# Layer 0's last stage with an interleaved order for VectorE and ScalarE, and the first values by pairs of token tiles

## The chip, the cores and the metric

The kernel runs on one core of a Trainium2 chip. The metric is the device time of one execution in microseconds; the median of several runs is compared.

## What is computed

Two layers of a decoder over 512 tokens with 1024 features, in 32-bit floats. Layer 0 mixes tokens by windowed attention and a short convolution, layer 1 by gated linear attention (GLA). Each layer then has a gated MLP and a per-layer embedding, which is the stage in question for layer 0:

```python
def _per_layer_embedding(x, p_i, norm, w_gate, w_proj):
    gate = jax.nn.sigmoid(_rms_norm(x, norm) @ w_gate)
    return gate * (p_i @ w_proj)

x = x + _per_layer_embedding(x, p[i], ...)          # end of layer 0
h = _rms_norm(x, mix_norm[1])                        # begin of layer 1
q, k, v, g_lr, og = _split(h @ w_in, GLA_SPLITS)
```

## The kernel before

Features lie on the 128 partitions: `xT[0..7]` are eight tiles of 128 features by 512 tokens. TensorE multiplies in a format that keeps only the upper part of a number, so every operand is cut in two: ScalarE writes the rounded part (`h`, an ACTIVATE Copy), VectorE the rest (`l = x - h`, a TENSOR_TENSOR subtract), and a product takes three matmuls (h·h, h·l, l·h). `mm3_rests_last` does those that need the weights' rest after all the others, so that the rest may come later.

`ple0` is layer 0's per-layer embedding. Its gate's weight matrix is worked in four groups of 256 output features (`for g in range(groups)`). A group's product with the tokens is made by a scheme of seven block products instead of eight: VectorE forms differences of the weight blocks in place in `raw` (`first_forms` L874 and L875, `second` L1410, `fourth` L1413), and `cut_blocks` (L850 ScalarE, L851 VectorE) cuts each form as it is ready. Per group there are four cuts: `plain`, `t13`, `t2` and `last`. The products build up in three PSUM banks: `bank` (from `pa`, its right half becomes `more`), `X` and `Y` (from `ps`). ScalarE copies one bank into another where a sum is used twice (L1420, L1421, L1487, L1503). `proj` multiplies p by its own weights into `pa` banks, two for a group. There are four `pa` and four `ps` banks.

The gate of a group is finished one group later (`late`): `closing` scales X and Y by the row norm R (L1428 to L1430, VectorE), `sigmoids` (L1435, ScalarE), `closed` multiplies by the projection (L1439, which frees its `pa` bank) and adds to `xT` (L1442). `squares` then prepares the next norm (L307, L311 ScalarE, L312 VectorE into `acc`). After the loop the last group is closed, `enter` scales and cuts the `xT` tiles for layer 1 (L113 ScalarE, L114 VectorE), and `cut` (L151, L152) cuts the first two weight blocks of the GLA values, `first_values`.

Inside `ple0` the order on TensorE, VectorE and ScalarE is the order in which the code is written (`manual_schedule`): each engine takes its instructions in that order and waits at each for what it needs. Outside, in `mixer1`, a planner orders each engine's instructions by its own costs; its order is fixed when the kernel is built.

`mixer1` begins with `Values(...).step(0)` and `step(1)`: the products of the eight token tiles with the two first weight blocks into four `ps` banks, one for each 128 tokens, all matmuls without the weights' rest ahead of those with it. Then come `spread` (R by transposes, L369), copies of the values out of PSUM (L1760, L1761, ScalarE), and `query(w, 0, turn_low)`, whose weights are cut by L151 and L152 and which calls `turn_low` (transposes of the gate's low rank, L1827) ahead of its last two feature tiles. `gate_up` loads the gate's small matrix `wgu` by ScalarE's DMA queue into the buffer that `acc` had, and rounds it (L1819, L1820). `acc` is summed by four transposes (L351) and a reduction (L360).

Of the kernel before, what the change touches and what calls it, by code (L numbers as in the profile page):

```python
# [63 lines left out]
class Kernel:  # L64
# [69 lines left out]
    def cut(self, rv, by, offs=(0, 0)):  # L134


        nc = self.nc
        na, nb = rv.shape[1:]
        parts = []
        n = 2 if na * nb > 1024 else 1  # L140
        for k in range(n):
            if by == "b":
                a, b = na, nb // n
                v = rv[:, :, k * b : (k + 1) * b]
            else:
                a, b = na // n, nb
# [4 lines left out]
            nc.scalar.activation(hv, v, AF.Copy)  # L151
            self.rest_cut = nc.vector.tensor_tensor(lv, v, hv.bitcast(F32), ALU.subtract)  # L152
            parts.append((hv, lv))
# [21 lines left out]
    def mm3_rests_last(self, terms, start, stop, weights, **kw):  # L175


        mm = self.nc.tensor.matmul
        begun, left = set(), {}
        for out, lt, rt in terms:  # L180
            left[id(out)] = left.get(id(out), 0) + 1
        for out, (lh, ll), (rh, rl) in terms:
            first = start and id(out) not in begun
            begun.add(id(out))
            mm(out, lh, rh, start=first, stop=False, **kw)  # L185
            lt, rt = (lh, rl) if weights == 0 else (ll, rh)
            mm(out, lt, rt, start=False, stop=False, **kw)  # L187
        for out, (lh, ll), (rh, rl) in terms:
            left[id(out)] -= 1
            lt, rt = (ll, rh) if weights == 0 else (lh, rl)  # L190
            mm(out, lt, rt, start=False, stop=stop and not left[id(out)], **kw)  # L191
# [648 lines left out]
    def cut_blocks(self, src, wide=True):  # L840

        nc = self.nc
        if wide:
            h, l = self.weight_tiles(BLOCKS)
        else:
            h, l = (
                self.sp.tile([P, S + 64], F32R, tag="sq", name=self.nm("t2"), bufs=2)[:, o : o + S] for o in BLOCKS
            )
        h, l = (x.rearrange("p (j n) -> p j n", n=src.shape[2]) for x in (h, l))
        nc.scalar.activation(h, src, AF.Copy)  # L850
        nc.vector.tensor_tensor(l, src, h.bitcast(F32), ALU.subtract)  # L851
# [521 lines left out]
    def ple0(self, fp, both, gain, next_gain):  # L1373
# [34 lines left out]

        def second(ev, od):
            tt(ev[:, :, :P], od[:, :, P:], ev[:, :, :P], ALU.subtract)  # L1410
# [4 lines left out]
        def begun(plain, rests_last):  # L1415
# [3 lines left out]
            X, Y = self.ps(), self.ps()  # L1419
            copy(X[:, left], bank[:, left])  # L1420
            copy(Y[:, left], bank[:, left])  # L1421
            return X, Y, bank[:, right]

        def closing(X, Y, more):
            gates = both()
            h2 = lambda x: x.rearrange("p (u t) -> p u t", u=2)
            g0, g1 = gates[:, 0], gates[:, 1]
            tt(g0, X, R, ALU.mult)  # L1428
            tt(h2(g1), h2(Y), more.unsqueeze(1).to_broadcast([P, 2, H]), ALU.add)
            tt(g1, g1, R, ALU.mult)  # L1430
            return g0, g1

        def sigmoids(gates):
            for s in gates:
                nc.scalar.activation(s, s, AF.Sigmoid)  # L1435

        def closed(g, gates, pjs):
            for s, pj in zip(gates, pjs):
                tt(s, s, pj, ALU.mult)  # L1439
            for c, s in enumerate(gates):  # L1440
                m = 2 * g + c
                tt(self.xT[m], self.xT[m], s, ALU.add)  # L1442
# [6 lines left out]
        with tc.manual_schedule(engines={ET.PE, ET.DVE, ET.Activation}):  # L1449
# [19 lines left out]
            X, Y, V = begun(plain, False)  # L1469
# [6 lines left out]
            for g in range(groups):  # L1476
                ends = g + 1 == groups
                product(V, t13, 0, x["s1"], False, g > 0)
# [3 lines left out]
                if g == 0:  # L1482
                    for m in (6, 7):
                        self.squares(m, spare())
                last = self.cut_blocks(od)
                product(Y[:, left], t2, 0, x["s2"], False, g > 0)
                copy(X[:, right], Y[:, left])  # L1487
                if late:
                    gates = closing(*late[1])
# [5 lines left out]
                else:  # L1495
                    pjs = [proj(2 * g), proj(2 * g + 1)]
                if not ends:
# [5 lines left out]
                copy(Y[:, right], X[:, right])  # L1503
                done = late
                if late:
                    closed(late[0], gates, late[2])
                late = g, (X, Y, more), pjs
                bank = X, Y
# [10 lines left out]
                product(bank[1][:, left], last, 1, x["s4"], False, g > 0)  # L1519
                product(bank[0][:, right], last, 0, x["o2"], False, g > 0)  # L1520
                if g == 0:
                    R = self.spread()
                if not ends:
                    if g + 2 < groups:
                        following = load(g + 2)
                    second(ev, od)
                    t2 = self.cut_blocks(ev[:, :, :P], False)
                    fourth(ev, od)
            raws = []
# [3 lines left out]
            ws = [self.cut(raws[0], "a")]  # L1533
            gates = closing(*late[1])
            sigmoids(gates)
            closed(late[0], gates, late[2])
            enter(4, 5)
            for m in (6, 7):
                self.squares(m, spare())
            ws.append(self.cut(raws[1], "a"))  # L1540
            enter(6, 7)
            self.first_values = ws
# [185 lines left out]
    def mixer1(self):  # L1728
# [4 lines left out]
        with tc.tile_pool(name="m1", bufs=1) as mp:  # L1733
# [5 lines left out]
            class Values:  # L1739


                def __init__(v, c0, c1, vn, ws=None):
                    v.c0, v.n, v.vn = c0, c1 - c0, vn
                    v.ws = ws or [
# [3 lines left out]
                def step(v, i):  # L1748
                    c0, n, vn = v.c0, v.n, v.vn
                    if i == 0:  # L1750
                        v.pss = [self.ps() for _ in range(NT)]
                    outs = [x[:, :n] for x in v.pss]
                    terms = [
                        (outs[t], tok(k, t), v.ws[i](k % 4, 0, n)) for k in range(4 * i, 4 * i + 4) for t in range(NT)
                    ]
# [12 lines left out]
            def feature(w, c, amid=None):  # L1768
# [3 lines left out]
                self.mm3_rests_last(terms[:n], True, n == ND, 0)  # L1772
                if amid:
                    amid()
# [428 lines left out]
```

## Time and profile before

| | us |
|---|---|
| median of 3 runs | 1209.86 (1209.41 to 1212.33) |
| the profiled execution | 1209.54 |
| its span in the profile | 1207.8 |
| the stage, from the loop's first product to the first values' product | 524.07 to 583.44 |
| the first values, to the first query's product | 583.44 to 603.47 |

In a timeline a row has the start, the duration, the engine, line and operation, the output and inputs, the shape and the count; in brackets the engine's idle time ahead of it and what ended that. PE is TensorE, DVE VectorE, ACT ScalarE, POOL GpSimd. A row with a count merges neighbours. In the rows of windows each engine has its busy time and instructions, and the last three numbers are the granted TensorE clock as a share, the DMA engines' busy share and GB/s.

### The profile page before, as it was taken

Reading aid. Unit: us, or ns where it says so; the run is one execution under the profiler, and the core shown is the slowest. Engines: PE = TensorE matmul, PEld = TensorE weight load, DVE = VectorE, ACT = ScalarE, POOL = GpSimd, SP = SyncE. Lnnn points to the kernel's source line nnn. Section 1 sums busy time; section 2 is a strip of 40 time slices with the busy share of each in tenths; the row PEclk is TensorE's granted clock in tenths of the full one; section 3 lists DMA queues with packets and bytes.
Section 4 is the critical chain, followed back from the end, with each engine's and each line's share of the span. In section 5 each row is a group of like instructions: output and inputs, shape, how many; then the busy total and the mean of one; then the engine's idle time right before and its main releaser. Section 6 shows DMA issues by size and latency. Waiting matters only on the chain.

```text
span 1207.8 us, 20228 instructions
## 1 busy us (share of the span) xinstructions
PE 1191.7 (99%) x8218; PEld 1083.1 (90%) x8218; DVE 994.7 (82%) x1593; ACT 692.3 (57%) x1137; POOL 45.4 (4%) x64
## 2 busy tenths in 40 slices
PE   9999999999999999998899999999999999999998
PEld 8877789999999889888888988889999999888887
DVE  6786687898999986987879876687989999988595
ACT  7466555656565644754573565555565656645374
POOL 2600000000000000000100000000000000000000
PEclk9999999999999999999999999999999999999999
DMA  7232222323232433321331322223333332422601
GB/s 221 73 102 72 73 88 71 113 98 112 99 106 88 157 122 97 99 68 61 114 93 47 94 71 70 87 70 106 106 106 106 101 110 95 141 88 97 209 1 70
DMA packets 112929, 117.76 MB, mean 98 GB/s; under 512 B 2840, under 2 KB 107858, under 8 KB 112836
## 3 DMA queue, kind: packets, MB, share of 16 engines
q1 hardware_dynamic: 112000, 115.88, 29.8%
q8 instruction: 64, 1.05, 0.4%
q0 software_dynamic: 560, 0.42, 0.3%
q14 instruction: 29, 0.24, 0.1%
q10 hardware_dynamic: 276, 0.18, 0.0%
HBM read 114.37 MB, written 2.10 MB: 96 GB/s over the span
## 4 chain that ended last, share of the span: by engine, by line
PE 85%; DVE 9%; ACT 3%; issue 1%; DMA 1%; POOL 0%; ACTq 0%; DVEq 0%
PE ps L171 8%; PE ps L172 7%; PE ps L173 7%; PE pa L172 6%; PE pa L173 6%; PE pa L171 6%; PE ps L903 5%; PE ps L905 5%; PE ps L904 5%; PE ps L185 4%; PE ps L187 4%; PE ps L191 4%; PE pa L903 2%; PE pa L905 2%; PE pa L904 2%; DVE wl L851 2%
## 5 line engine op out<-in xcount | busy, mean ns | idle before, releaser
L152 DVE TENSOR_TENSOR wl<-raw,wh 128x1024 fp32r<-128x1024 f32 (+4 forms) x142 | 162.4, 1146 | 44.2 <-ACT wh L151 40.7
L151 ACT ACTIVATE wh<-raw 128x1024 fp32r<-128x1024 f32 (+4 forms) x142 | 140.9, 996 | 69.8 <-PE ps L172 28.6
L850 ACT ACTIVATE wh<-raw 128x1024 fp32r<-128x1024 f32 x90 | 95.7, 1063 | 122.8 <-DVE raw L875 79.0
L966 DVE SCALAR_TENSOR_TENSOR zt<-z,vfa,zt 128x510 f32<-128x510 f32 (+1 forms) x176 | 130.8, 744 | 0.3
L851 DVE TENSOR_TENSOR wl<-raw,wh 128x1024 fp32r<-128x1024 f32 x90 | 110.0, 1222 | 24.3 <-ACT wh L850 23.4
L173 PE MATMUL pa<-b,wl 128*128 128x256 f32 x352 | 97.3, 276 | 0.1
L173 PE MATMUL pa<-a,wl 128*128 128x256 f32 x352 | 97.2, 276 | 0.0
L171 PE MATMUL pa<-a,wh 128*128 128x256 f32 x352 | 97.2, 276 | 0.0
L171 PE MATMUL pa<-b,wh 128*128 128x256 f32 x352 | 97.2, 276 | 0.0
L172 PE MATMUL pa<-b,wh 128*128 128x256 f32 x352 | 97.2, 276 | 0.0
L172 PE MATMUL pa<-a,wh 128*128 128x256 f32 x352 | 97.2, 276 | 0.0
L964 ACT ACTIVATE zt<-z,vfb 128x512 f32<-128x512 f32 x88 | 71.3, 810 | 18.1 <-DVE z L956 9.1
L185 PE MATMUL ps<-b,wh 128*128 128x512 f32 (+1 forms) x200 | 76.5, 385 | 0.2 <-ACT vt L1761 0.2
L187 PE MATMUL ps<-b,wh 128*128 128x512 f32 (+1 forms) x200 | 75.2, 379 | 0.0
L173 PEld LDWEIGHTS pa<-b,wl 128*128 128x128 f32 x352 | 66.1, 188 | 0.2 <-DVE wl L152 0.2
L171 PEld LDWEIGHTS pa<-a,wh 128*128 128x128 f32 x352 | 66.1, 188 | 0.0
L171 PEld LDWEIGHTS pa<-b,wh 128*128 128x128 f32 x352 | 66.1, 188 | 0.0
L172 PEld LDWEIGHTS pa<-a,wh 128*128 128x128 f32 x352 | 66.1, 188 | 0.0
L172 PEld LDWEIGHTS pa<-b,wh 128*128 128x128 f32 x352 | 66.1, 188 | 0.0
L173 PEld LDWEIGHTS pa<-a,wl 128*128 128x128 f32 x352 | 66.1, 188 | 0.0
L903 PE MATMUL ps<-four,wh 128*128 128x256 f32 x232 | 64.7, 279 | 0.0
L905 PE MATMUL ps<-four,wl 128*128 128x256 f32 x232 | 64.1, 276 | 0.0
(525 smaller groups left out, 3710.9 us busy)
## 6 DMA issues: line engine op xcount, KB each, us to landing
raw<-in_ffn_w_up_dram SPq DMA_DIRECT2D x42, 1024.0 KB, 5.0
raw<-in_ffn_w_down_dram SPq DMA_DIRECT2D x13, 1024.0 KB, 5.0
raw<-in_hy_w_in_dram SPq DMA_DIRECT2D x8, 1024.0 KB, 5.2
raw<-in_gla_w_in_dram SPq DMA_DIRECT2D x8, 1024.0 KB, 5.2
raw<-in_ffn_w_down_dram SPq DMA_DIRECT2D x8, 768.0 KB, 4.8
raw<-in_ple_w_gate_dram SPq DMA_DIRECT2D x6, 1024.0 KB, 6.5
raw<-in_hy_w_out_dram SPq DMA_DIRECT2D x16, 256.0 KB, 4.1
raw<-in_gla_w_out_dram SPq DMA_DIRECT2D x4, 1024.0 KB, 5.0
```

What stands on the lines that cost most here:

```text
L151: nc.scalar.activation(hv, v, AF.Copy)
L152: self.rest_cut = nc.vector.tensor_tensor(lv, v, hv.bitcast(F32), ALU.subtract)
L171: mm(out, lh, rh, start=start, stop=False, **kw)
L172: mm(out, lh, rl, start=False, stop=False, **kw)
L173: mm(out, ll, rh, start=False, stop=stop, **kw)
L185: mm(out, lh, rh, start=first, stop=False, **kw)
L187: mm(out, lt, rt, start=False, stop=False, **kw)
L850: nc.scalar.activation(h, src, AF.Copy)
L851: nc.vector.tensor_tensor(l, src, h.bitcast(F32), ALU.subtract)
L903: mm(out, wh, xh, start=first and j == 0, stop=False, **kw)
L905: mm(out, wl, xh, start=False, stop=j == ND // 2 - 1, **kw)
L966: nc.vector.scalar_tensor_tensor(out=y[:, tap:], in0=z[:, : S - tap], scalar=w[:, f : f + 1], in1=y[:, tap:], op0=ALU.mult, op1=ALU.add,)
```

## The change

The written order in `ple0` changes, and with it the helpers: `closing`, `sigmoids` and `closed` fall apart into single steps. `cut_blocks` and `cut` take a function `amid` whose instructions stand between ScalarE's rounding and VectorE's rest.

- The late group's first gate multiplication and its sigmoid go into the middle of the cut `last`.
- The multiplications by the projection go ahead of the next group's two first block differences.
- The late group's additions go into the middle of the cut `t13`, and ScalarE's two copies of the new bank go behind that cut's rounding.
- The squares go behind `second`; for the last two tiles behind the last `enter`.
- After the loop, the last group's gate goes into the middle of the first cut of the values' weights.
- `Values.step(0)` of the first values goes over token tiles 0 and 1 for all four features, then 2 and 3. `turn_low` may be issued only after the matmuls written ahead of it.

TensorE's written order in `ple0` stays, and so does the number of instructions. In `mixer1` the planner's order moves in a few places: on ScalarE the rounding of the first query's weights (L151) now stands behind the roundings of `wgu`, all eight copies of the values and the copy of R, where it stood ahead of the copies; on VectorE its rest stands behind the low rank's buffers; on TensorE the four transposes of `acc` stand behind 25 matmuls of `step(1)`, before behind 8, and the four low-rank transposes stand together inside the first query.

```diff
-    def cut_blocks(self, src, wide=True):
+    def cut_blocks(self, src, wide=True, amid=None):
...
         nc.scalar.activation(h, src, AF.Copy)
+        if amid:
+            amid()
         nc.vector.tensor_tensor(l, src, h.bitcast(F32), ALU.subtract)
...
+                if late:
+                    before, (Xb, Yb, mb), pjb = late
+                    gates = both()
+
+                    def amid():
+                        tt(gates[:, 0], Xb, R, ALU.mult)
+                        sigmoid(gates[:, 0])
+                else:
+                    squared(ND // 2 - 1)
-                last = self.cut_blocks(od)
+                last = self.cut_blocks(od, True, amid)
                 product(Y[:, left], t2, 0, x["s2"], False, g > 0)
                 copy(X[:, right], Y[:, left])
                 if late:
-                    gates = closing(*late[1])
+                    summed(gates[:, 1], Yb, mb)
...
                 if not ends:
                     raw, ev, od = following
-                    plain = self.first_forms(ev, od, raw)
+                    plain = self.cut_blocks(raw[:, :, :P])
                 if late:
-                    sigmoids(gates)
+                    sigmoid(gates[:, 1])
+                    for c in range(2):
+                        tt(gates[:, c], gates[:, c], pjb[c], ALU.mult)
+                if not ends:
+                    first_third(ev, od)
                 product(X[:, right], t13, 1, x["s3"], False, g > 0)
                 copy(Y[:, right], X[:, right])
...
                 if ends:
+                    added(before, gates)
                     pjs.append(proj(2 * g + 1))
+                    squared(before)
+                    enter(0, 1, 2, 3)
                 else:
-                    X, Y, V = begun(plain, True)
-                    t13 = self.cut_blocks(ev)
-                if done:
-                    for m in (2 * done[0], 2 * done[0] + 1):
-                        self.squares(m, spare())
-                if ends:
-                    enter(0, 1, 2, 3)
+                    X, Y, bank = begun(plain, True)
+                    t13 = self.cut_blocks(ev, True, (lambda: added(before, gates)) if late else None)
+                    copies(X, Y, bank)
...
                     second(ev, od)
+                    if late:
+                        squared(before)
                     t2 = self.cut_blocks(ev[:, :, :P], False)
                     fourth(ev, od)
...
-            ws = [self.cut(raws[0], "a")]
-            gates = closing(*late[1])
-            sigmoids(gates)
-            closed(late[0], gates, late[2])
+            before, (Xb, Yb, mb), pjb = late
+            gates = both()
+            ws = [self.cut(raws[0], "a", amid=lambda: (tt(gates[:, 0], Xb, R, ALU.mult), summed(gates[:, 1], Yb, mb)))]
+            for c in range(2):
+                sigmoid(gates[:, c])
+                tt(gates[:, c], gates[:, c], pjb[c], ALU.mult)
+            added(before, gates)
             enter(4, 5)
-            for m in (6, 7):
-                self.squares(m, spare())
             ws.append(self.cut(raws[1], "a"))
             enter(6, 7)
+            squared(before)
...
+                    if v.given and i == 0:
+                        order = [(k, t) for u in (0, 2) for k in ks for t in (u, u + 1)]
...
-                    amid()
+                    with tc.issue_after(end.ins):
+                        amid()
```

`added` holds the two additions to `xT`, `squared` the two squares, `summed` the sum with `more` and its scaling by R, `first_third` the two differences that `first_forms` made.

More of the change, by code (lines that the diff above doesn't have):

```diff
@@ L190, in mm3_rests_last @@
             lt, rt = (ll, rh) if weights == 0 else (lh, rl)
-            mm(out, lt, rt, start=False, stop=stop and not left[id(out)], **kw)
+            end = mm(out, lt, rt, start=False, stop=stop and not left[id(out)], **kw)
+        return end
     def rsqrt(self, out, src, scale):
@@ L1418, in begun, with copies, summed, sigmoid @@
             product(bank[:, left], plain, 0, x["e1"], True, rests_last)
-            X, Y = self.ps(), self.ps()
+            return self.ps(), self.ps(), bank
+        def copies(X, Y, bank):
             copy(X[:, left], bank[:, left])
             copy(Y[:, left], bank[:, left])
-            return X, Y, bank[:, right]
-        def closing(X, Y, more):
-            gates = both()
+        def summed(s, Y, more):
             h2 = lambda x: x.rearrange("p (u t) -> p u t", u=2)
[L1427 to L1440, printed above, removed]
+            tt(h2(s), h2(Y), more.unsqueeze(1).to_broadcast([P, 2, H]), ALU.add)
+            tt(s, s, R, ALU.mult)
+        def sigmoid(s):
+            nc.scalar.activation(s, s, AF.Sigmoid)
+        def added(g, gates):
+            for c in range(2):
                 m = 2 * g + c
-                tt(self.xT[m], self.xT[m], s, ALU.add)
+                tt(self.xT[m], self.xT[m], gates[:, c], ALU.add)
+        def squared(g):
+            for m in (2 * g, 2 * g + 1):
+                self.squares(m, spare())
         raw, ev, od = load(0)
@@ L1468, in ple0 @@
                               s3=parts(bh)[0], s4=parts(bh)[1]))
-            X, Y, V = begun(plain, False)
+            X, Y, bank = begun(plain, False)
+            copies(X, Y, bank)
             tt(s34[:, right], o[:, left], s12[:, right], ALU.subtract)
@@ L1477, in ple0 @@
                 ends = g + 1 == groups
+                V = bank[:, right]
                 product(V, t13, 0, x["s1"], False, g > 0)
@@ L1532, in ple0 @@
                 nc.sync.dma_start(raws[-1], wv[:, k0 : k0 + 4, 1696:2064])
-            ws = [self.cut(raws[0], "a")]
-            gates = closing(*late[1])
-            sigmoids(gates)
-            closed(late[0], gates, late[2])
+            before, (Xb, Yb, mb), pjb = late
+            gates = both()
+            ws = [self.cut(raws[0], "a", amid=lambda: (tt(gates[:, 0], Xb, R, ALU.mult), summed(gates[:, 1], Yb, mb)))]
+            for c in range(2):
+                sigmoid(gates[:, c])
+                tt(gates[:, c], gates[:, c], pjb[c], ALU.mult)
+            added(before, gates)
             enter(4, 5)
-            for m in (6, 7):
-                self.squares(m, spare())
             ws.append(self.cut(raws[1], "a"))
             enter(6, 7)
+            squared(before)
             self.first_values = ws
@@ L1743, in __init__ @@
                     v.c0, v.n, v.vn = c0, c1 - c0, vn
+                    v.given = ws is not None
                     v.ws = ws or [
```

36 lines of the change are left out of this document (22 added, 14 removed).

## The prediction

> **What bounds the kernel now.** I read the page's first part, then the chain that ended last, then the stretches of ten microseconds around the stage, then the timeline of each engine inside it.
>
> ```profile
> span 1207.8 us, 20228 instructions
> ...
> PE 1191.7 (99%) x8218; PEld 1083.1 (90%) x8218; DVE 994.7 (82%) x1593; ACT 692.3 (57%) x1137; POOL 45.4 (4%) x64
> ...
> PE 85%; DVE 9%; ACT 3%; issue 1%; DMA 1%; POOL 0%; ACTq 0%; DVEq 0%
> ```
>
> TensorE sets the time: it is busy for 99% of the span, and only 1207.8 - 1191.7 = 16.1 us of idle time exist anywhere. So the change can give only what TensorE idles or crawls in the stretch that it touches, and whatever it takes it takes there. TensorE's rows around that stretch with idle time ahead of them, its last matmuls ahead of the first one, and two of the ten-microsecond windows:
>
> ```profile
> 545.43 0.39 PE L191 MATMUL ps<-b,wl 128*128 128x256 f32 x2
> 547.62 0.39 PE L185 MATMUL pa<-a,wh 128*128 128x256 f32 x1 [1.80 <-DVE zt L1439]
> ...
> 562.89 0.56 PE L185 MATMUL pa<-a,wh 128*128 128x256 f32 x1 [2.66 <-DVE zt L1439]
> ...
> 577.96 0.39 PE L185 MATMUL ps<-a,wh 128*128 128x256 f32 x1 [0.74 <-ACT ps L1503]
> ...
> 583.44 0.67 PE L185 MATMUL ps<-wh,b 128*128 128x368 f32 x1 [2.47 <-ACT wh L151]
> ```
> ```profile
> 560.00:570.00 10.00, 7.34 (x50) 7.13 (x50) 6.99 (x10) 3.31 (x7) 0.00 (x0) 0.83 0.15 56
> ...
> 580.00:590.00 10.00, 7.53 (x39) 7.33 (x38) 9.76 (x16) 7.10 (x12) 0.00 (x0) 0.83 0.15 47
> ```
>
> Four stalls, 7.67 us. The last two rows have the granted clock as the third number from the end: 0.83 over ten microseconds, which at half speed is 3.4 us, so 1.7 us of matmul time is lost behind each of the two longest stalls (2.66 and 2.47), and none behind the 1.80. That is 7.67 + 3.4 = 11.1 us, the most that this change could ever bring. A closed stall gives some 0.16 more than its figure, since idle time is counted from the end of a matmul and the next could start before it (two take 0.39 us, one 0.28).
>
> **The change, part by part.** *Group 2 of the loop.* The stall of 2.66 us ends with VectorE's first multiplication by the projection (L1439), which frees the bank that the next group starts in. VectorE's rows:
>
> ```profile
> 546.89 1.28 DVE L1439 TENSOR_TENSOR zt<-zt,pa 128x512 f32<-128x512 f32 x2
> ...
> 550.95 1.23 DVE L851 TENSOR_TENSOR wl<-raw,wh 128x1024 fp32r<-128x1024 f32 x1 [1.58 <-ACT wh L850]
> 552.09 0.69 DVE L312 TENSOR_TENSOR acc<-acc,so 128x512 f32<-128x512 f32 x1
> 552.69 0.68 DVE L1410 TENSOR_TENSOR raw<-raw 128x512 f32<-128x512 f32 x1
> 554.07 0.69 DVE L851 TENSOR_TENSOR t<-raw,t 128x512 fp32r<-128x512 f32 x1 [0.70 <-ACT t L850]
> 554.68 0.68 DVE L1413 TENSOR_TENSOR raw<-raw 128x512 f32<-128x512 f32 x1
> 556.49 1.23 DVE L851 TENSOR_TENSOR wl<-raw,wh 128x1024 fp32r<-128x1024 f32 x1 [1.13 <-ACT wh L850]
> 557.64 0.68 DVE L1428 TENSOR_TENSOR zt<-ps,R 128x512 f32<-128x512 f32 x1
> 558.24 0.68 DVE L1429 TENSOR_TENSOR zt<-ps,so 128x512 f32<-128x512 f32 x1
> ...
> 560.82 0.69 DVE L874 TENSOR_TENSOR raw<-raw 128x512 f32<-128x512 f32 x1
> ...
> 562.15 1.28 DVE L1439 TENSOR_TENSOR zt<-zt,pa 128x512 f32<-128x512 f32 x2
> ```
>
> L1413 ends at 555.36 and L1439 starts at 562.15: 6.79 us. The gate's first multiplication (L1428, 0.60 from start to start) goes into the 1.13 us wait, and the two block differences (L874 and the next, 562.15 - 560.82 = 1.33) go behind L1439: 6.79 - 0.60 - 1.33 = 4.86 us. From the first L1439 of the group before (546.89, 15.26 us earlier) to L1413's end are 8.47 us. There the two differences come in (+1.33), and two waits nearly go: the 1.58, because ScalarE now rounds before it copies TensorE's new bank, and the 0.70, because the sum of squares (L312) moves into it. 8.47 + 1.33 - 1.54 - 0.65 = 7.6. VectorE's cycle becomes 7.6 + 4.9 = 12.5 us in place of 15.26. TensorE's own work between the two stalls is 562.89 - 547.62 - 2.66 - 0.16 = 12.45. The two tie: the stall falls from 2.66 to about 0 (0 to 0.5, as nothing is spare), and with it the 1.7 us of slow clock.
>
> *Group 1.* The same saving, but the sigmoid's table load comes earlier on ScalarE:
>
> ```profile
> 540.14 1.06 ACT L850 ACTIVATE wh<-raw 128x1024 fp32r<-128x1024 f32 x1 [0.78 <-DVE raw L1413]
> ...
> 543.06 1.28 ACT L1435 ACT_TABLE_LOAD   x1
> 544.35 1.15 ACT L1435 ACTIVATE zt<-zt 128x512 f32<-128x512 f32 x2
> ```
>
> After the rounding (ends 541.20) come the load (1.28), one sigmoid (0.58), the copy for TensorE's next product (0.3, an estimate from half the size of a 0.58 us sigmoid) and only then the next group's rounding (1.06): 544.4. Its rest on VectorE (1.2) and the multiplication (0.68) end at 546.25, against 547.6. The stall falls by 1.4, to 0.4.
>
> *Group 3.* The copy that ends the 0.74 us stall waited behind the second sigmoid; with the gate's first multiplication in VectorE's wait it comes 0.6 us sooner after L1413, and L1413 itself comes sooner by the waits above: closed. The group's other copy now stands behind the first sigmoid, with one projection to cover it instead of two. Counted from L1439's start, L1413 ends at 7.6 + 0.6 (this group adds two sums of squares, not one) = 8.2, the rounding ends at 9.3, the sigmoid at 9.9, the copy at 10.2. TensorE starts at 0.73 and has 72 matmuls at 0.113 (0.39 - 0.28 and a little) and a projection of 1.4 to do, 10.3. So it is covered by 0.1 us; without that cover it would cost up to 0.3.
>
> *Up to the first GLA values.* This stall I expect to stay. Its chain is untouched: additions, squares, four roundings, the weights' rounding, and TensorE.
>
> ```profile
> 578.27 1.29 DVE L1442 TENSOR_TENSOR xT<-xT,zt 128x512 f32<-128x512 f32 x2
> ```
> ```profile
> 580.13 2.55 ACT L113 ACTIVATE b<-xT,vec 128x512 fp32r<-128x512 f32 x4
> 582.58 1.51 ACT L151 ACTIVATE wh<-raw 128x736 fp32r<-128x736 f32 x2
> ```
>
> From the first addition to TensorE's start are 583.44 - 578.27 = 5.17 us. The addition comes 0.6 us sooner after L1413, but TensorE comes out of group 3 sooner as well: 2.4 us of stall against 2.47, and the clock drops again. The order by pairs moves few matmuls (the scheduler had nearly that order) and costs nothing. So the values start at 583.44 - 1.4 - 2.7 - 1.7 - 0.74 - 0.1 - 0.5 (three times 0.16) = 576.3: 7.1 us gained.
>
> *Behind the values: a wait takes the place.* Two things move. The squares of the last two tiles now follow their roundings, so that the transposes that sum them go from 8 matmuls into the second half of the values to 25, and all that hangs on them comes 17 of them later against TensorE: at (2.86 - 0.33) / 15 = 0.17 us each, by the first row below with one matmul's 0.33, 2.9 us. And ScalarE's queue changes: rounding the first query weights stood ahead of the eight copies of the values; in the new order it is behind them, behind two roundings of the gate weights and behind the copy of R.
>
> ```profile
> 590.44 2.86 PE L191 MATMUL ps<-wl,b 128*128 128x368 f32 x16
> ...
> 594.48 0.60 PE L351 MATMUL pa<-cf,acc 128*128 128x128 f32 x4
> ...
> 601.63 0.60 PE L369 MATMUL pa<-cf,rtok 128*128 128x128 f32 x4
> ...
> 603.47 0.50 PE L185 MATMUL ps<-b,wh 128*128 128x512 f32 x1 [0.17 <-ACT vt L1761]
> ```
> ```profile
> 600.44 0.63 ACT L1819 ACTIVATE wgs<-wgu 64x512 fp32r<-64x512 f32 x1 [7.08 <-DMA wgu<-in_gla_w_gate_up_dram]
> 600.98 1.04 ACT L151 ACTIVATE wh<-raw 128x1024 fp32r<-128x1024 f32 x1
> 602.05 0.63 ACT L1820 ACTIVATE wgs<-wgu 32x512 fp32r<-32x512 f32 x1
> 602.70 0.27 ACT L1760 ACTIVATE glr<-ps,rtok 128x16 f32<-128x16 f32 x1
> ...
> 605.08 0.64 ACT L371 COPY R<-pa 128x512 f32<-128x512 f32 x1
> 605.55 2.08 ACT L151 ACTIVATE wh<-raw 128x1024 fp32r<-128x1024 f32 x2
> ```
>
> Call TensorE's spread (601.63) S. The first copy cannot start before the values of tile 0 are complete, S - 0.3. Four copies take half of 605.08 - 602.70, 1.2 us: S + 0.9. There stands the gate weights' rounding, which waits for its load: 600.44 - 595.08 = 5.36 us after the transposes, now at S - 3.9, so S + 1.5. Then 0.54 and 0.63 for the two roundings, 1.2 for the four other copies, 0.5 for R, 1.04 for the query weights: S + 5.4. TensorE's query started at 603.47 - 601.63 = S + 1.84. Loss 3.6 us. TensorE then idles 4.9 us (S + 0.5 to S + 5.4), twice the stalls that cost it its clock, so add 1.7. The gate's low-rank transposes stand together inside the query now, where one stood ahead of it: 0.1 as an estimate.
>
> *Sum.* S comes 7.1 sooner; 7.1 - 3.6 - 1.7 - 0.1 = 1.7 us. The profiled execution took 1209.54 (span 1207.8 and 1.7 around it), the median of the runs is 1209.86. Behind the query the order of all engines is as before and TensorE runs without a gap, so the 1.7 stays: 1207.8 for a profiled execution, 1208.1 against the median.
>
> A rule that weighs on this: the Trainium skill, "TensorE: Matmul & The Clock Gate", section "Why this matters for your kernels", wants no idle gaps over some 3 us, and its section "What's actually happening" tells of a free-running window of 3413 ns. This trace is harsher than the 3 us (2.47 and 2.66 dropped the clock, 1.80 did not), but a window that does not follow the kernel would make the 2.4 us stall a matter of where it falls; that is the second case below.
>
> **The rivals.** *The clock stays up before the values.* 2.4 lies between 1.80 (no drop) and 2.47 (drop). Without a drop 1.7 us more are gained: 1206.4, and with the 0.5 us by which the load's wait could be shorter, 1205.9. For: the stall is the shortest that would still drop. Against: 2.47 is much nearer than 1.80.
>
> *No new wait behind the values.* If ScalarE were through its queue by S + 1.8 the whole 7.1 would stay, 1202.8; half of it 1205. Against: the instructions are in one queue and sum to more than 5 us.
>
> *The gate weights' load decides (slower than before).* ScalarE stands still until that load lands, with the query's weights behind it. Each microsecond beyond S + 1.5 costs one. It breaks even 1.7 us late. Were the load to sit behind one 1 MB load of weights,
> ```profile
> raw<-in_gla_w_in_dram SPq DMA_DIRECT2D x8, 1024.0 KB, 5.2
> ```
> 5.2 us, the time would be 1208.1 + 5.2 = 1213.3. Against: it shared the engines with such a load before, too.
>
> *The stalls stay.* If TensorE's bank is freed by the second multiplication, or ScalarE's new order holds the sigmoid back, groups 1 and 2 keep about a stall of over 2 us with its slow clock: 3 to 4 us less, 1211 to 1212.
>
> **How the numbers follow.** About 0.3% (3.6 us) is what a measurement of this kernel can tell from no change: faster is below 1206.2, slower above 1213.5. Forecast 0.52; clock up 0.22; no new wait 0.08; load 0.08; stalls stay 0.10. Faster: half of the clock case, most of no new wait, some of the forecast's edge, 0.24. Slower: half of the load case and a little of the last, 0.06. Same 0.70. The forecast's own range is 1206.5 to 1209.5; to hold 8 in 10 it reaches to 1205.0 for the clock case and to 1211.5 for the stalls.
>
> **What would show it.** Right: idle before the new group's start under 0.5 us in groups 1 and 2, granted clock 1.00 there; 2.2 to 2.6 us before the values; a gap near 4.9 us before the first query, ended by ScalarE's rounding of its weights, with half clock behind it. Wrong: no such gap, or the stalls by the projection's bank still there.

## The result, and the profile after

The changed kernel takes 1207.84 us (median of 20 runs, 1206.33 to 1210.36), the kernel before 1209.96 (20 runs beside it, 1208.8 to 1212.54). The ratio is 0.998, 95% interval 0.9974 to 0.9987: a gain of 2.1 us, below the 3.6 us that the prediction took as measurable for a single comparison, and shown by the interval all the same. The profiled executions took 1209.54 before and 1207.74 after.

The page's first part and its chain by engines:

```profile
span 1206.0 us, 20223 instructions
...
PE 1189.8 (99%) x8218; PEld 1081.3 (90%) x8218; DVE 995.2 (83%) x1593; ACT 692.8 (57%) x1137; POOL 45.9 (4%) x64
...
PE 85%; DVE 10%; ACT 3%; issue 1%; DMA 1%; POOL 0%; ACTq 0%; DVEq 0%; POOLq 0%
```

TensorE's idle time in the whole span went from 16.1 us to 1206.0 - 1189.8 = 16.2. Nothing was gained there in sum; the gain of 1.8 us in these two executions is in TensorE's busy time (1191.7 to 1189.8), most of it because 3.8 us of its work ran at half clock in place of 6.8. Where the idle time lies is quite another matter. TensorE's timeline (start, duration, and in brackets the idle time ahead and who ended it):

```profile
546.44 0.36 PE L191 MATMUL pa<-a,wh 128*128 128x256 f32 x1 [0.62 <-DVE zt L1524]
...
558.62 0.39 PE L197 MATMUL ps<-b,wl 128*128 128x256 f32 x2
558.86 0.36 PE L191 MATMUL pa<-a,wh 128*128 128x256 f32 x1
...
576.49 0.43 PE L191 MATMUL ps<-wh,b 128*128 128x368 f32 x1 [2.26 <-ACT wh L151]
...
593.14 0.60 PE L376 MATMUL pa<-cf,rtok 128*128 128x128 f32 x4
599.60 0.79 PE L191 MATMUL ps<-b,wh 128*128 128x512 f32 x1 [5.86 <-ACT wh L151]
```

Group 1's stall of 1.80 us is 0.62, group 2's 2.66 has no bracket any more, group 3's is gone, the one before the values is 2.26, and between TensorE's spread (593.14) and the first query there is a new gap of 5.86 us. The clock, as the third number from the end, by stretches:

```profile
560.00:570.00 10.00, 10.00 (x84) 9.74 (x83) 9.30 (x14) 5.55 (x10) 0.00 (x0) 1.00 0.04 4
...
576.00:593.00 17.00, 16.51 (x100) 16.48 (x101) 14.69 (x22) 7.45 (x13) 3.93 (x7) 1.00 0.42 130
593.00:610.00 17.00, 11.14 (x45) 8.55 (x44) 7.10 (x8) 10.74 (x20) 0.00 (x0) 0.80 0.28 89
```

The stretch of group 2's old stall (560 to 570) and the values (576 to 593) ran at full clock; in the last stretch 17 x 0.20 / 0.5 = 6.8 us were at half clock. Read in short windows, that is 596.58 to 603.41: the second half of the gap and the first 3.8 us of the queries. Of the 20 runs the four longest (1208.91 to 1210.36) have a mean granted clock of 0.995, the others 0.996 to 0.998, so in some executions the clock may have dropped once more than in this one.

In balance, by the starts of the same rows: the values begin 583.44 - 576.49 = 6.95 us earlier, the spread 601.63 - 593.14 = 8.49 (the clock did not drop behind the 2.26 us), the first query 603.47 - 599.60 = 3.87. From there to the gate's product it takes 8.59 us in place of 6.69, with the half clock in it, which leaves the 2.0 seen at that product (610.16 before, 608.19 after).

What holds the query, in the chain that ended last (start, length, engine, tile and line):

```profile
587.87 0.70 DVE acc L319
...
588.68 1.01 POOL run L2097
...
590.21 0.46 POOL wgu L1841
590.69 0.32 ACTq L1843
591.04 4.43 DMA wgu<-in_gla_w_gate_up_dram
```

and ScalarE's timeline:

```profile
592.99 0.27 ACT L1787 ACTIVATE glr<-ps,rtok 128x16 f32<-128x16 f32 x1 [8.33 <-PE ps L197]
...
595.48 0.63 ACT L1847 ACTIVATE wgs<-wgu 64x512 fp32r<-64x512 f32 x1 [1.16 <-DMA wgu<-in_gla_w_gate_up_dram]
...
597.99 0.59 ACT L378 COPY R<-pa 128x512 f32<-128x512 f32 x1
598.46 2.03 ACT L151 ACTIVATE wh<-raw 128x1024 fp32r<-128x1024 f32 x2
```

The query weights' rounding (L151 at 598.46) is the last of ScalarE's queue, behind eight copies of the values, a wait for the gate weights' load, two roundings and the copy of R. GpSimd clears two other tiles (from 588.68) before it clears `wgu`, and only then is the load asked for; before, those two were cleared (592.83 to 593.76) ahead of the transposes.

### The profile page after: what moved, and what is told of

It is laid out like the page before. It is cut to its first block, busy times and chain, and to the rows that moved or that the text cites. A ratio compares the mean times of both kernels' runs of the same rounds, so it can differ in the third digit from the quotient of the medians.

```text
span 1206.0 us, 20223 instructions
## 1 busy us (share of the span) xinstructions
PE 1189.8 (99%) x8218; PEld 1081.3 (90%) x8218; DVE 995.2 (83%) x1593; ACT 692.8 (57%) x1137; POOL 45.9 (4%) x64
## 4 chain that ended last, share of the span: by engine, by line
PE 85%; DVE 10%; ACT 3%; issue 1%; DMA 1%; POOL 0%; ACTq 0%; DVEq 0%; POOLq 0%
PE ps L177 8%; PE ps L178 8%; PE ps L179 8%; PE pa L179 6%; PE pa L178 6%; PE pa L177 6%; PE ps L912 5%; PE ps L914 5%; PE ps L913 5%; PE ps L191 4%; PE ps L193 4%; PE ps L197 4%; PE pa L912 2%; PE pa L914 2%; PE pa L913 2%; DVE wl L860 1%
## 5 line engine op out<-in xcount | busy, mean ns | idle before, releaser
L151 ACT ACTIVATE wh<-raw 128x1024 fp32r<-128x1024 f32 (+4 forms) x142 | 140.8, 996 | 70.0 <-PE ps L178 28.5
```

## The experiments

Theory A, the prediction's: the loop's order closes the stalls, and the gain is given back because the squares of the last two tiles, now behind the splits, make the planner put the query weights' rounding last on ScalarE. The rivals: the loop's edits themselves gain little; the pairs order or the call that holds the transposes is what moved the planner's order; or (C) the gate weights' load sets the query's start, whatever the order. The times come from four rounds, each with the kernel before beside it, whose median was 1209.5 to 1210.0; so differences of a few tenths between kernels of different rounds say nothing.

**The multiplications by the projection back behind the block differences.**

```diff
                     sigmoid(gates[:, 1])
-                    for c in range(2):
-                        tt(gates[:, c], gates[:, c], pjb[c], ALU.mult)
                 if not ends:
                     first_third(ev, od)
+                if late:
+                    for c in range(2):
+                        tt(gates[:, c], gates[:, c], pjb[c], ALU.mult)
```

> The changed kernel with the multiplications by the projection behind the next group's two block differences again, all else as changed. Theory A (this order is two thirds of what closes the stalls, 1.33 us of VectorE in each group): the stall of group 1 grows from 0.6 to 1.9, that of group 2 from 0 to about 1.3, no drop of the clock, 1207.8 + 2.6 = 1210.4 us. Theory E (filling VectorE's wait with the gate's first multiplication is what closes them): within 0.7 us of 1207.8.

Measured: 1209.7 (12 runs, ratio to before 1.0, 0.9992 to 1.0009): the whole gain of the change is gone. TensorE's timeline of this kernel:

```profile
547.05 0.55 PE L191 MATMUL pa<-a,wh 128*128 128x256 f32 x1 [2.06 <-DVE zt L1527]
...
561.90 0.35 PE L191 MATMUL pa<-a,wh 128*128 128x256 f32 x1 [0.67 <-DVE zt L1527]
...
578.17 0.44 PE L191 MATMUL ps<-wh,b 128*128 128x368 f32 x1 [0.85 <-ACT wh L151]
```

Group 1's stall returns (2.06, with 3.4 us of half clock behind it), group 2's is 0.67, and the one before the values shrinks to 0.85, since TensorE itself now comes later. Values start 578.17 - 576.49 = 1.7 us later and the medians differ by 1.9, where 2.6 was expected of theory A and under 0.7 of its rival. The total gain is gone, yet not all of the loop's: the values still start 583.44 - 578.17 = 5.3 us earlier than before. So this edit is worth 1.7 of the 6.95 us; which of the loop's other edits brought the rest was not tried one by one. The kernel also shows that one stall hides the next.

**The squares ahead of the second cut.**

```diff
             enter(4, 5)
+            squared(before)
             ws.append(self.cut(raws[1], "a"))
             enter(6, 7)
-            squared(before)
```

> The changed kernel with the squares of the last two tiles put back ahead of the second cut of the values' weights. With that alone the planner's order on ScalarE behind the values is the old one again (the first query's weights are rounded ahead of the eight copies) and the transposes that sum the squares stand behind 8 matmuls of the second half, not 25. Theory A (the queue order behind the values is what takes the gain back, and it hangs on where the squares stand): the gap before the first query falls from 5.9 us to about 1.5, no slow clock behind it, 1207.8 - 4.5 - 1.7 = 1201.5 us. Theory B (the new order in the loop itself makes ScalarE late for the values' copies): the gap stays over 4 us, 1207 us or more.

Measured: 1203.4 (6 runs, ratio 0.9954, 0.9939 to 0.9968), 4.4 us below the changed kernel. ScalarE's timeline, then TensorE's:

```profile
593.20 0.63 ACT L1847 ACTIVATE wgs<-wgu 64x512 fp32r<-64x512 f32 x1 [6.92 <-DMA wgu<-in_gla_gate_bias_dram]
593.74 1.04 ACT L151 ACTIVATE wh<-raw 128x1024 fp32r<-128x1024 f32 x1
```
```profile
596.23 0.50 PE L191 MATMUL ps<-b,wh 128*128 128x512 f32 x1 [0.88 <-ACT vt L1788]
```

The order on ScalarE is the old one again (gate weights, query weights, then the copies) and the query starts 1.5 us behind the spread (594.75) in place of 6.5. The time is 1.9 above the expected: in the profiled execution the clock dropped behind the stall of 2.25 us before the values, which it did not do in the changed kernel's. The times spread from 1202.87 to 1207.64, and why they spread so far is not shown.

**The query weights' load and rounding given priority, and nothing else.**

```diff
-            w = pair_w(0)
+            with tc.high_priority(offset=150):
+                w = pair_w(0)
```

> The changed kernel with a higher priority for the load and the cuts of the first query's weights, nothing else: on ScalarE their two roundings come ahead of all copies of the values, in the middle of the gate weights' five loads; the squares and the transposes stay late, so the load of the gate weights lands as late as before or later. Theory A (the place of the rounding in the queue): the query waits only for the first copy of the values, gap under 1 us, 1207.8 - 5.3 - 1.7 = 1200.8 us. Theory C (the late landing of the gate weights' load is the wait, whatever stands in the queue): the gap stays near 5.9 us and the time within 1 us of 1207.8.

Measured: 1201.76 (5 runs, ratio 0.9932, 0.992 to 0.9944): 6.1 us below the changed kernel. ScalarE and TensorE:

```profile
593.12 1.06 ACT L151 ACTIVATE wh<-raw 128x1024 fp32r<-128x1024 f32 x1 [7.57 <-DVE rs L205]
...
596.66 0.63 ACT L1847 ACTIVATE wgs<-wgu 64x512 fp32r<-64x512 f32 x1 [0.32 <-DMA wgu<-in_gla_w_gate_up_dram]
```
```profile
595.78 0.50 PE L191 MATMUL ps<-b,wh 128*128 128x512 f32 x1 [0.39 <-ACT vt L1788]
```

Here the rounding that waits for the gate weights' load starts 1.9 us behind the spread (594.79; 2.3 in the changed kernel), and the query starts before it, 1.0 us behind the spread. So C falls: the load delays the query only because the query weights stand behind it in ScalarE's queue.

The same line in the kernel before:

> The kernel before, with the query weights' roundings given the same priority that gained 6 us in the changed kernel. Theory: there the queries wait only 1 us in all behind the values (0.79 for the low-rank copy, 0.17 for the values' copy) at full clock, so it gains at most that: 1209.0 to 1209.8. Rival: the priority helps by itself, whatever the loop does: 1204 or less.

Measured: 1210.97 (11 runs, ratio 1.0014, 1.0005 to 1.0023): slower by 1.4 us, outside of what either expected. TensorE, then ScalarE:

```profile
603.62 0.28 PE L1827 MATMUL pa<-cf,glr 128*16 128x128 f32 x1 [1.79 <-ACT glr L1760]
```
```profile
600.62 1.99 ACT L151 ACTIVATE wh<-raw 128x1024 fp32r<-128x1024 f32 x2
```
```profile
600.00:610.00 10.00, 8.05 (x34) 6.29 (x33) 4.69 (x5) 7.12 (x14) 0.00 (x0) 0.83 0.54 173
```

Both halves of the query weights now go ahead of the first low-rank copy, whose transpose stands ahead of the query on TensorE: 0.79 us of waiting became 1.79, and in this execution the clock dropped behind it as well (0.83 over ten microseconds, 1.7 us lost), which it does not do there in the kernel before. (This execution took 1213.87, so it stands for more than the 1.4 us of the median.) The priority is no gain in itself; it mends an order that the change brought about.

**TensorE kept busy in the gap** with 24 products that nothing uses, to price the half clock by itself.

```diff
             R = self.spread()
+            warm = self.pa()
+            for _ in range(24):
+                nc.tensor.matmul(warm, xg[0][0][:, :P], xg[0][0], start=True, stop=True)
             w = pair_w(0)
```

> The changed kernel with 24 matrix products on data already there (128x512, result not used) between the spread and the query weights' first product, to keep TensorE busy through the gap of 5.86 us; the order on every other engine is unchanged. Theory A: of the 4.6 us lost behind the values, the gap itself is the wait for ScalarE's rounding and stays, but the half clock that followed it (3.8 us of work at half speed behind the start of the queries) goes, so 1.8 us less: 1206.0. Rival: the query weights' later halves set the pace there, so that the half clock costs nothing: 1207.8.

Measured: 1204.84 (5 runs, ratio 0.9963, 0.9949 to 0.9976), 3.0 us below the changed kernel where 1.8 was expected. TensorE, and the clock:

```profile
592.94 5.70 PE L2105 MATMUL pa<-b 128*128 128x512 f32 x24
599.04 0.50 PE L191 MATMUL ps<-b,wh 128*128 128x512 f32 x1 [0.40 <-ACT wh L151]
...
601.89 1.53 PE L197 MATMUL ps<-b,wl 128*128 128x512 f32 x6
```
```profile
590.00:600.00 10.00, 9.60 (x49) 8.14 (x48) 2.66 (x4) 6.36 (x14) 2.03 (x4) 1.00 0.35 115
600.00:610.00 10.00, 10.00 (x46) 7.90 (x46) 5.02 (x6) 6.71 (x10) 0.00 (x0) 1.00 0.43 126
```

From the query's start to its first rests are 601.89 - 599.04 = 2.85 us, against 604.22 - 599.60 = 4.62 in the changed kernel: 1.77, close to the 1.7 that the prediction put on the half clock. The profiled executions differ by 3.2. Of the rest, 0.57 is there before the gap (group 1 starts at 545.87 in place of 546.44), and 0.84 lies in layer 1, between the spread at 819.46 (821.80) and the transposes at 1150.92 (1154.10), which no edit touches. The thirteen other kernels, the one before among them, take 331.8 to 334.3 us for that stretch, this one 331.5. So this part of the difference is hardly more than what the stretch scatters by from execution to execution, and it is not shown to be a gain of the filled gap.

**The loop's order alone, and each of the two small edits by itself.** One kernel has neither the pairs order of the first values nor the call that holds the low-rank transposes behind the query's sixth term; one lacks the call, one lacks the pairs.

```diff
-                    if v.given and i == 0:
-                        order = [(k, t) for u in (0, 2) for k in ks for t in (u, u + 1)]
...
-                    with tc.issue_after(end.ins):
-                        amid()
+                    amid()
```

> The changed kernel without its two edits to the next stage: the first values go over all four token tiles again, and the low-rank transposes may be issued ahead of the query's matmuls. The order on ScalarE behind the values is that of the changed kernel. Theory A: these two edits are worth nothing, 1207.8 us within 0.5. Theory D (the edits to the next stage are what disturbs it): under 1205 us.

> The changed kernel without the call that holds the low-rank transposes behind the first query part's sixth term; the pairs order stays. The planner then puts the four transposes at the spread, into the gap. If the transposes are where the kernel with the loop alone got its 1.75 us: 1206.1 (query start 0.2 us earlier or the same, no transposes and no gate products late in the query stretch, half clock over earlier). If it was the values' pairs order: 1207.8.

> The changed kernel with the first values in the old order (one row tile after another, four token tiles each); the transposes stay held behind the sixth term. Theory: the pairs hide nothing, since the values' weights and tiles are there in either order once the stall before them ends: 1207.8. From the two kernels without the holding call, with pairs 1206.74 and without 1206.09, the difference would make 1207.2. Rival: the pairs cover the wait for the second rows of tiles; without them the values stall by 0.7 to 1.3 us more: 1208.5 to 1209.

Measured: without both 1206.09 (5 runs, ratio 0.9967, 0.9955 to 0.9978), without the call 1206.74 (9 runs, 0.9973, 0.9963 to 0.9983), without the pairs 1207.55 (11 runs, 0.9984, 0.9976 to 0.9993), with both 1207.84. The pairs are worth nothing that shows. The call costs 1.1 to 1.5 us by the medians, though the intervals overlap a little. TensorE of the kernel without both:

```profile
593.28 0.27 PE L1852 MATMUL pa<-cf,glr 128*16 128x128 f32 x1
...
599.35 0.80 PE L191 MATMUL ps<-b,wh 128*128 128x512 f32 x1 [1.50 <-ACT wh L151]
```

The query weights are still rounded last, so neither edit is what moved the planner's order. The transposes fall into the gap, where they cost nothing; in the changed kernel they cost 605.96 - 605.60 = 0.36 us inside the query. From query to first rests it takes 603.64 - 599.35 = 4.29 in place of 4.62, since the half clock ends 3.1 us behind the query's start (at 602.46) in place of 3.8. Both, with a query that starts 0.25 earlier, make 0.9 of the 1.75 us; the remainder I can't place.

**The stall before the values.** With the priority above, ScalarE rounds the first half of the values' weights after two splits instead of four; in a second kernel the squares of group 2 go behind it as well (`between` is the splits of tiles 2 and 3, `late0` is group 2).

```diff
-                    enter(0, 1, 2, 3)
+                    enter(0, 1)
...
             nc.scalar.activation(hv, v, AF.Copy)
+            if between and k == 0:
+                between()
```
```diff
-                    squared(before)
                     enter(0, 1)
...
+            squared(late0)
```

> The kernel with the query weights' roundings ahead (1201.8), and in the last group ScalarE rounds the first half of the values' weights after the splits of two token tiles instead of four. Theory: the stall of 2.25 us before the first values was ScalarE's row of splits, so it shrinks by two splits, to 1.0 us, and at 1.0 us the clock does not drop behind it (1.7 us more): 1198.9. Rival: the weights' load lands only when ScalarE gets there now, so the stall stays 2.2 and the time 1201.8. Between them, stall shorter but the clock drops all the same: 1200.6.

> As the one before, and the squares of group 2's two tiles go behind the rounding of the values' weights on both engines (they stood ahead of the splits: 1.2 us on ScalarE, 1.5 us on VectorE). Theory: the stall before the values closes to 0.3 us or to the landing of the weights' load, whichever is later; VectorE's sum of work is the same: 1198.2. Rival: the squares now delay the last group's multiplications and with them the splits of the last two tiles, and the values stall later by as much: 1199 to 1200.

Measured: 1201.79 (5 runs, ratio 0.9932, 0.9919 to 0.9944) and 1200.86 (5 runs, 0.9928, 0.9915 to 0.994). TensorE of the first, then of the second:

```profile
574.86 0.43 PE L193 MATMUL ps<-wh,b 128*128 128x368 f32 x1 [1.02 <-ACT wh L151]
...
594.29 0.50 PE L193 MATMUL ps<-b,wh 128*128 128x512 f32 x1 [1.33 <-ACT vt L1791]
```
```profile
582.89 0.77 PE L195 MATMUL ps<-wh,b 128*128 128x368 f32 x3 [0.58 <-DVE b L114]
...
594.33 0.50 PE L193 MATMUL ps<-b,wh 128*128 128x512 f32 x1 [2.07 <-ACT vt L1792]
```

The stall became 1.0 as expected, and in the second kernel it closed; the times did not follow. The query starts at 594.3 in both: what the values gain, the gap behind them takes (0.39, then 1.33, then 2.07 us, with 3.4 us of half clock behind the last). In the second kernel's chain VectorE's last sum of squares (to 587.89) releases GpSimd's clearing, that the issue of the `wgu` load on ScalarE's queue, and this stands ahead of the query weights' rounding (591.67) and the copies. Which of these rows would move the query's start was not tried. The expected gain turned into the next wait.

**The masks' load behind the query weights' load.** The masks had the buffer that the first half of the values' weights leaves, and the query weights' load had to wait for the next one: it was issued at 585.87, and at 581.12 with the edit.

```diff
+            w = pair_w(0)
             mf = self.raw(7, P)
             nc.sync.dma_start(mf, a["cst_m"].rearrange("p (a b) -> p a b", b=P))
...
             R = self.spread()
-            w = pair_w(0)
```

Once as the only edit, and once with the second cure (without its priority) and the splits and squares of the last two tiles ahead of the values' second rests on VectorE.

> The changed kernel with one thing moved: the query weights' load is asked for ahead of the masks' load instead of behind it, so that it gets the buffer that the first half of the values' weights leaves at about 580 instead of the one that the masks or the second half hold until 587. Nothing is given priority by hand. Theory: the gap of 5.9 us behind the values is only the place of the query weights' rounding on ScalarE; with the load early the planner puts the rounding ahead of the gate-weights' and the values' copies, the queries start within 0.5 us of the spread, and the half clock behind the gap goes with it: 5.5 and 1.8 less, 1200.5. Rival: VectorE now has the query weights' rest (1.2 us) ahead of the norm's reduction, the spread is later by as much: 1201.7.

> The masks' load behind the query weights' load, together with the earlier rounding of the values' weights and the squares of group 2 behind it (the second cure), and the splits and squares of the last two tiles ahead of the values' second rests on VectorE. Theory: values start without a stall, the norm's reduction comes 1.7 us earlier on VectorE, the query weights are rounded before the spread, so that the waits of 0.33 and 2.07 us that the second cure kept behind the values go, and no gap is left behind which the clock drops: 1200.9 less 2.4 and some: 1198.2. Rival: VectorE's sum of work is the bound behind the values and gives the same end in every order: 1200.5.

Measured: 1202.58 (5 runs, ratio 0.9943, 0.993 to 0.9955) and 1199.39 (5 runs, 0.9923, 0.991 to 0.9935). ScalarE and TensorE of the first, TensorE and the clock of the second:

```profile
586.45 1.06 ACT L151 ACTIVATE wh<-raw 128x1024 fp32r<-128x1024 f32 x1 [0.34 <-PE ps L197]
```
```profile
595.36 0.60 PE L376 MATMUL pa<-cf,rtok 128*128 128x128 f32 x4
596.25 0.50 PE L191 MATMUL ps<-b,wh 128*128 128x512 f32 x1 [0.29 <-ACT vt L1788]
```
```profile
593.06 0.50 PE L193 MATMUL ps<-b,wh 128*128 128x512 f32 x1 [0.54 <-ACT vt L1790]
```
```profile
570.00:580.00 10.00, 10.00 (x68) 9.76 (x68) 9.77 (x15) 8.80 (x15) 0.00 (x0) 1.00 0.25 75
580.00:590.00 10.00, 9.48 (x58) 9.09 (x57) 9.89 (x15) 5.34 (x8) 2.42 (x6) 1.00 0.40 110
590.00:600.00 10.00, 9.40 (x48) 7.54 (x46) 5.09 (x8) 6.84 (x15) 1.01 (x1) 1.00 0.78 263
```

With the load early the planner itself puts the rounding first, and the query follows the spread by 0.9 us in place of 6.5: the third way to the same end, and like the squares' place it needs no hand on the priorities. It missed 1200.5 by 2.1. About half of that may again be a clock that dropped, as it did in the profiled execution behind 2.19 us before the values; at a mean clock of 1.00 it took 1201.43 and 1201.5, which is nearer to the rival's 1201.7. With the stalls cured too there is no drop in this stretch of the profiled execution, and TensorE is idle for 1.1 us in these thirty. The median of 1199.39 is the lowest here, 0.77% below the kernel before and 8.4 us below the changed one, and lies between the 1198.2 expected and the rival's 1200.5. (The profiled execution took 1201.74.) Against the second cure the intervals overlap nearly in full (0.991 to 0.9935, 0.9915 to 0.994), so a gain over it is not shown, and the loads' order and VectorE's were not tried apart.

## Why the prediction was right, point by point

*The loop.* VectorE's cycle was put at 12.5 us. Its timeline after:

```profile
545.61 1.28 DVE L1524 TENSOR_TENSOR zt<-zt,pa 128x512 f32<-128x512 f32 x2
...
558.03 1.28 DVE L1524 TENSOR_TENSOR zt<-zt,pa 128x512 f32<-128x512 f32 x2
```

558.03 - 545.61 = 12.42, and the stall of group 2 is gone with its slow clock. Group 1 was put at 0.4 and is 0.62, a little over the 0.5 named as the sign of being right; group 3 closed. That the multiplications' place carries a part of this is shown by moving them back: the stalls are 2.06 and 0.67 then.

*Up to the values.* A stall of 2.4 at 576.3 was forecast; it is 2.26 at 576.49. The step that failed is the clock behind it: it was forecast to drop, and in the profiled execution did not. This was the first rival's mechanism, worth 1.7 us, though not by the rival's reason: the length of 2.26 us did not decide it (the last section has what did).

*Behind the values.* The new wait is there, at ScalarE, behind the queue that the prediction wrote out, and the half clock behind it costs 1.77 by the kernel that fills the gap, against 1.7. Mis-sized was the wait: 4.6 us lost in place of 3.6. The term is the load's S + 1.5 (S is the start of TensorE's spread, 593.14), which is S + 2.34 (595.48 - 593.14). Its 5.36 us from the end of the transposes were taken from the trace of before; after, they are 595.48 - 589.44 = 6.04, because GpSimd clears the scan's tiles first and starts on `wgu` 0.70 us behind the transposes instead of 0.05: a queue that the prediction did not look at. The transposes themselves came 0.2 later against the spread than worked out.

*The sum.* Plus 1.7 for the clock, less 1.0 for the wait, 0.2 for the values' start and 0.3 for the transposes inside the query (0.36 measured, 0.1 estimated): errors of opposite sign that nearly cancel, and 1207.84 against 1208.1. The mechanism was right and carried the forecast; that it agrees to 0.3 us is partly luck.

*The rivals.* That no wait takes the place is what six of the kernels above make true or nearly so, three of them by a single edit, at 1199.4 to 1203.4; the three lie at 1201.8 to 1203.4, near the 1202.8 worked out for it. The load as the bound was refuted by the priority alone. Nearest to the stalls that stay is the kernel with the multiplications moved back, 1209.7 with one stall of over 2 us, where 1211 to 1212 was worked out for both groups.

## What to carry to other kernels

A stall that is closed shows the next one, so follow the chain past the edit: here 7 us won in a loop were mostly lost some 25 us later, in a part that a planner orders and that one moved pair of squares had reordered. When such a gain is missing, look for the row that ends the new gap, and ask which of what stands ahead of it on its queue it does not need; a load asked for earlier, or one priority, gave back 5 to 6 us. And list every queue that a moved load stands in, the one that clears its tile as well.

## What the runs showed of the hardware

The half clock does not follow the length of a stall alone. Of the seven stalls of 2.25 or 2.26 us ahead of the values, with the same instructions ahead of them, two were followed by half clock and five (the changed kernel among them) were not. Stalls of 2.06, 2.07, 2.19, 2.46 and 2.65 us were followed by it, those of 1.80 and 1.82 were not, but the 1.79 in the kernel before with the priority was.

What decides is where a stall falls on a grid. In every trace here a half clock in the middle of the kernel lasts 3.41 us or twice that. Within one execution its starts lie 20.48 us apart before (562.94, 583.42), twice 20.48 in the kernel before with the priority (563.70, 584.18, 604.66) and 51.20 with the multiplications moved back (547.06, 598.26): 6, 6, 6 and 15 times 3.413. Carried back by six such steps from 596.58, the changed kernel's grid has an edge at 576.10, inside its stall (574.23 to 576.49). With the squares moved, the edge at 576.66 lies just behind the stall. TensorE's busy time is the second number; the clock is again the third from the end:

```profile
572.69:576.10 3.41, 1.54 (x14) 1.34 (x12) 3.29 (x5) 3.41 (x6) 0.00 (x0) 1.00 0.01 3
576.10:579.51 3.41, 3.02 (x18) 3.02 (x19) 3.38 (x6) 2.38 (x5) 0.00 (x0) 1.00 0.00 0
```
```profile
573.25:576.66 3.41, 1.16 (x11) 0.97 (x10) 3.31 (x6) 3.41 (x7) 0.00 (x0) 1.00 0.00 0
576.66:580.07 3.41, 3.41 (x12) 3.41 (x13) 3.38 (x6) 2.37 (x5) 0.00 (x0) 0.50 0.00 0
```

In the windows of these traces that were followed by half clock TensorE was busy for 1.61 us or less (1.46 behind the stall of 1.79); in those around a stall that were not, for 1.54 or more. So a window idle for a little over half of its 3.41 us was enough, and a stall of 2.26 us that an edge cuts in two was not. (The busy times end at modelled ends of matmuls, so the border between 1.54 and 1.61 is not sharp.) The Trainium skill, "TensorE: Matmul & The Clock Gate", section "What's actually happening", tells of a free-running window of 3413 ns, and the grid agrees. Its table puts the drop behind at least one idle window of some 3.4 us; here 1.95 us of idle time in one (3.41 - 1.46) were enough.

A gap that can't be closed can be made cheaper: 24 products without a use in it kept the clock up and took 1.77 us off the work behind.
